# First mixture of experts: products in two halves of 32 slots, the second half and the shared block under three short branches

## The chip, the cores and the metric

The kernel runs on one core of one Trainium2 chip, in one launch. The metric is the device time of a launch in microseconds; the median of several runs counts. The core's engines are named as in the profile: PE is TensorE's matmuls (PEld its weight loads), DVE is VectorE, ACT ScalarE, POOL GpSimd, and SP SyncE, whose queue issues the weight transfers. A "q" behind an engine's name (PEq, SPq) is its sequencer. PSUM is where PE writes its results.

## The reference

The model has two layers over 256 context and 256 latent tokens of width 1024. Each layer ends in a mixture of 32 experts; every token goes to the two best experts of its group, and each expert is a gated MLP with a hidden width of 512:

```python
def run(args):
    xe, e = args
    return (jax.nn.silu(xe @ w_gate[e]) * (xe @ w_up[e])) @ w_down[e]
...
gates = gw * p_in / jnp.sum(p_in, axis=-1, keepdims=True)
eidx = grp[:, None] * MOE_PER_GROUP + e_in.astype(jnp.int32)
```

The first layer's mixture, which the change concerns, sees all 512 tokens, so 1024 pairs of token and expert; the second layer's sees the 256 latent tokens. How many tokens an expert gets is known only on the chip, from the router.

## The kernel before

**Slots.** The first mixture is `experts()`, called for layer 0. An expert has 64 slots. Tokens are put into them by a product with a one-hot matrix (`onehot`, `gather`, L1935), and the results are spread back to the tokens by another (`scatter`, L2002, then DVE at L2004 and L2006). What an expert has beyond 64 tokens goes to a shared block of 64 more slots `xx`; that block is computed with the weights of every expert that is too large, under a branch on the expert's flag (`shared`, L2197). A loop behind it (`others`) would take further shared blocks if one didn't do.

**One expert.** The order on each engine is the order in which the code is written. For expert e: `stage1` (L1958) multiplies the 64 gathered tokens by the gate and up weights, half of the depth at a time, each in a column group of 64 slots and 512 columns, with a piece of an earlier pair's scatter between the halves. Then comes the branch with `shared`. Behind it are `hidden` (silu on ACT, L1962, and the product with gate and up on DVE, L1963), the second product of expert e − 1 (`products`, `stage2`, L1979), `parts` (which splits its result into a high and a low part for an exact scatter: a copy on ACT, L1986, and a subtraction on DVE, L1987, twice), another piece of scatter, the transposes of the hidden values (`hidden_t`, L1971, L1973), a gather for the next group of four experts, and every second or fourth expert `turned` (L1993) and `gates_of` (L1947).

**Weights.** The `stream` holds tiles of 1 MiB in a ring; in this mixture it has 11 slots. An expert takes six: two of gate, two of up, two of down. `stream.give(n)` returns n tiles and lets SP ask for the next n in the plan. In `experts` this is `give(6)` after the second product; behind the last expert's tiles the plan goes on with the next layer's `od_w_in`.

**Branches.** A `tc.If` is run by every engine: it loads the flag (`values_load`), compares, and jumps over the body when the flag is zero. The branch at the last expert holds two more, nested: the shared block for expert 0, whose weights are long gone and are loaded again, and `others()` with loads for all 32 experts.

**Bookkeeping.** The flags are worked out on DVE in small steps (`bookkeeping`) during expert 0, in tiles borrowed from ones used later.

**The second mixture**, `narrow()`, is not touched. It has 32 slots for an expert and four column groups of 32 slots and 256 columns (L2287 first product, L2304 second), one short branch for an expert at L2501, and one large one at L2479.

Of the kernel before, what the change touches and what calls it, by code (L numbers as in the profile page):

```python
# [206 lines left out]
class Kernel:  # L207
# [1404 lines left out]
    def moe_tiles(self, NT):  # L1612
# [8 lines left out]
            extra=mp.tile([128, NE + 1 if NT > 2 else 3 * NE + 1], I32, name="extra"))  # L1621
# [196 lines left out]
    def bookkeeping(self, gp, lgg, mg, m1, m2, ohg, masked, chosen, oh1, oh2, slots, blocks):  # L1818
# [33 lines left out]
        nc.vector.tensor_reduce(over, counts.rearrange("p t e -> p e t"), axis=AX.X, op=ALU.add)  # L1852
        nc.vector.tensor_scalar(over, over, float(slots), 0.0, op0=ALU.subtract, op1=ALU.max)
# [20 lines left out]
        flags = gp.tile([128, extra.shape[1]], F32, name="flags")  # L1874
# [8 lines left out]
        nc.vector.tensor_tensor(flags[:, 0:NE], flags[:, 0:NE], over, op=ALU.mult)  # L1883
        n = self.most_blocks(NT, blocks)
# [3 lines left out]
        at = 0 if blocks > 1 else NE - 1  # L1888
        for v in (more[:, 0:1], flags[:, 1 - (at > 0):2 - (at > 0)]):
            nc.vector.tensor_tensor(flags[:, at:at + 1], flags[:, at:at + 1], v, op=ALU.max)  # L1890
# [7 lines left out]
    def experts(self, L, x, seg, bookkeeping, ending):  # L1898

        nc, tc, c, stream, I = self.nc, self.tc, self.c, self.stream, self.I  # L1900
# [4 lines left out]
        GB = 4  # L1905
        with ExitStack() as st:
# [4 lines left out]

            place = cycle([(wp, "xg"), (self.xp, "x01")] if L else [(wp, "xg"), (wp, "xh")])
# [28 lines left out]
            def gates_of(b):  # L1941

                g2 = self.m["gate2"]
                ps = pp.tile([128, GB // 2, 2, 2], F32, name="b2")
                for i in range(GB // 2):
                    for t in range(NT):
                        nc.tensor.matmul(ps[:, i].rearrange("p h e -> p (h e)"), OH[b][:, t, 2 * i:2 * i + 2].rearrange("p e s -> p (e s)"),  # L1947
                                         g2[:, :, t, b * GB + 2 * i:b * GB + 2 * i + 2],
                                         start=i == 0 and t == 0, stop=t == NT - 1, skip_group_check=True)
                GS[b] = wp.tile([128, GB], F32, name="gs")  # L1950
                for j in range(2):
                    nc.vector.tensor_reduce(GS[b][64:128, j::2], ps[64 * j:64 * j + 64, :, :, j], axis=AX.X, op=ALU.add)
# [7 lines left out]
            def hidden(ps, gs):  # L1960
                sg, hs = low[:, 0:FE], low[:, FE:].rearrange("p (k q) -> p k q", k=4)
                nc.scalar.activation(sg[64:128], ps[0:64], AF.Silu)  # L1962
                nc.vector.scalar_tensor_tensor(  # L1963
                    hs[64:128].rearrange("s k q -> s q k"), ps[64:128].rearrange("s (q k) -> s q k", k=4), gs,
                    sg[64:128].rearrange("s (q k) -> s q k", k=4), op0=ALU.mult, op1=ALU.mult)
                return hs

            def hidden_t(hs, ht, tag=dict(name="b2")):
                pt = pp.tile([128, 4, SLOTS], F32, **tag)
                for k in range(4):  # L1970
                    nc.tensor.transpose(pt[:, k], hs[64:128, k], c["ident"][64:128, 64:128])  # L1971
                ht = ht.rearrange("p (k s) -> p k s", k=4)
# [3 lines left out]
            def stage2(ps, ht, w, half):  # L1976
                for k in range(2 * half, 2 * half + 2):
                    for j in range(2):
                        nc.tensor.matmul(ps[64 * j:64 * j + 64], ht[:, k], w[:, k % 2, 512 * j:512 * j + 512],  # L1979
                                         start=k == 0, stop=k == 3)  # L1980
# [619 lines left out]
```

## Time and profile before

| | us |
|---|---|
| median of 3 runs (lowest to highest) | 1871.91 (1870.68 to 1872.27) |
| the profiled execution | 1874.16 |
| its span, first to last instruction | 1872.4 |
| PE busy | 1637.9 (87%) |
| DVE busy | 817.3 (44%) |
| ACT busy | 447.0 (24%) |
| POOL busy | 139.5 (7%) |
| mean granted clock of PE | 0.925 |
| DMA, mean over the span | 270 GB/s |

The span is cut by what the kernel does: the first mixture runs from about 600 to 1155 us, the second from about 1400 to the end. A row of a timeline reads: start, length, engine, line, operation, output<-inputs, shapes, count of instructions merged into the row, and in brackets how long the engine sat idle before it and what ended that. "PEq L2197" as the releaser means that PE's own sequencer was at the branch of line 2197.

### The profile page before, as it was taken

To read this page: it belongs to the slowest core of one execution; us is meant where nothing else is said; L and a number is where in the kernel's file an instruction comes from. 1 tells how busy PE (TensorE), PEld (TensorE's weight loads), DVE (VectorE), ACT (ScalarE), POOL (GpSimd) and SP (SyncE) were. 2 spreads that over 40 slices of the span, in tenths; PEclk is the share of its full clock that TensorE was granted. 3 is DMA by queue.
4 is the path that set the end of the run, shared out by engine and by line. 5 is a ranking of instruction groups with operands and counts; after the bars stand their busy time and mean duration, and the time that the engine had idled before them with its cause. 6 is when DMAs were issued, how large, how long until landed. Compare 5 with 4: busy or idle time off the path is not lost. (4 is left out here: it accounts for less than half of the span.)

```text
span 1872.4 us, 31604 instructions
## 1 busy us (share of the span) xinstructions
PE 1637.9 (87%) x12958; PEld 933.3 (50%) x12958; DVE 817.3 (44%) x1622; ACT 447.0 (24%) x945; POOL 139.5 (7%) x170
## 2 busy tenths in 40 slices
PE   5988999989998999999999997999987787776667
PEld 2755556454776444444444433888754333332222
DVE  2564434544358245555555456665562212221113
ACT  3442222421213211111111112544421111111001
POOL 1021000103115000000000003200010000000001
PEclk8998987879898999999999997999988899898888
DMA  9275300652243879999999990622699998999996
GB/s 319 82 239 191 113 24 23 216 172 92 85 146 141 350 283 386 399 385 390 390 401 379 399 386 12 198 68 85 259 369 413 415 415 318 414 414 414 366 400 253
DMA packets 127284, 505.76 MB, mean 270 GB/s; under 512 B 11317, under 2 KB 38945, under 8 KB 85986
## 3 DMA queue, kind: packets, MB, share of 16 engines
q1 hardware_dynamic: 120946, 493.96, 68.1%
q0 software_dynamic: 3488, 8.26, 1.4%
q8 instruction: 143, 2.34, 0.5%
q10 hardware_dynamic: 2640, 0.65, 0.2%
q14 instruction: 67, 0.55, 0.1%
HBM read 501.73 MB, written 1.10 MB: 269 GB/s over the span
## 5 line engine op out<-in xcount | busy, mean ns | idle before, releaser
L1979 PE MATMUL b<-w,ht 128*64 128x512 f32 x512 | 118.8, 604 | 8.6 <-PEq L2197 8.2
L2004 DVE TENSOR_TENSOR tmp<-b,g 128x512 f32<-128x512 f32 x128 | 87.6, 686 | 70.1 <-PE b L2002 69.2
L1958 PE MATMUL b<-w,xh 128*64 128x512 f32 x512 | 116.9, 599 | 0.0
L1958 PE MATMUL b<-w,xg 128*64 128x512 f32 x512 | 116.9, 599 | 0.0
L2287 PE MATMUL b<-w,x 128*32 128x256 f32 x1024 | 77.8, 430 | 31.7 <-DMA w<-moe_w_up 14.9
L2006 DVE TENSOR_TENSOR x<-x,tmp 128x512 f32<-128x512 f32 x124 | 90.1, 726 | 4.3
L2287 PE MATMUL b<-w,xg 128*32 128x256 f32 x1024 | 74.0, 420 | 19.1 <-DMA w<-moe_w_up 14.4
L1987 DVE TENSOR_TENSOR yl<-b,yh 64x512 fp32r<-64x512 f32 x62 | 42.7, 688 | 101.4 <-ACT yh L1986 101.4
L2304 PE MATMUL b<-w,ht 128*32 128x256 f32 x1024 | 71.2, 415 | 16.6 <-ACT ht L2299 12.4
L2292 DVE SCALAR_TENSOR_TENSOR low<-b,gs,low 64x256 f32<-64x256 f32 x32 | 15.7, 490 | 157.6 <-ACT low L2291 157.6
L1979 PEld LDWEIGHTS b<-w,ht 128*64 128x64 f32 x512 | 41.6, 138 | 84.0 <-issue 72.5
L1962 ACT ACTIVATE low<-b 64x512 f32<-64x512 f32 x33 | 19.4, 588 | 253.9 <-PEq L2197 221.0
L2453 DVE COPY y<-b 32x256 f32<-32x256 f32 x62 | 25.9, 418 | 119.6 <-PE b L2304 106.3
L2287 PEld LDWEIGHTS b<-w,x 128*32 128x32 f32 x1024 | 37.1, 122 | 69.5 <-DMA w<-moe_w_up 20.6
L1986 ACT CAST yh<-b 64x512 fp32r<-64x512 f32 x62 | 36.0, 581 | 127.8 <-PE b L1979 104.6
L1963 DVE SCALAR_TENSOR_TENSOR low<-b,gs,low 64x512 f32<-64x512 f32 x32 | 36.1, 1127 | 67.2 <-ACT low L1962 67.2
L1958 PEld LDWEIGHTS b<-w,xh 128*64 128x64 f32 x512 | 33.9, 136 | 62.6 <-issue 62.0
L1958 PEld LDWEIGHTS b<-w,xg 128*64 128x64 f32 x512 | 33.9, 136 | 62.3 <-issue 61.3
L2291 ACT ACTIVATE low<-b 64x256 f32<-64x256 f32 (+1 forms) x36 | 14.4, 399 | 209.9 <-PEq L2501 130.4
L2287 PEld LDWEIGHTS b<-w,xg 128*32 128x32 f32 x1024 | 36.0, 120 | 53.3 <-DMA w<-moe_w_up 19.5
L2002 PE MATMUL b<-yh,oht 128*128 128x512 f32 (+1 forms) x128 | 58.3, 456 | 3.2 <-DVE tmp L2004 3.2
L1374 PE MATMUL b<-w,hH 128*128 128x256 f32 x320 | 59.4, 286 | 0.0
(868 smaller groups left out, 3115.5 us busy)
## 6 DMA issues: line engine op xcount, KB each, us to landing
w<-moe_w_gate SPq DMA_DIRECT2D x128, 1024.0 KB
w<-moe_w_up SPq DMA_DIRECT2D x128, 1024.0 KB
w<-moe_w_down SPq DMA_DIRECT2D x128, 1024.0 KB
w<-ada_w SPq DMA_DIRECT2D x48, 1024.0 KB
w<-od_w_in SPq DMA_DIRECT2D x12, 1024.0 KB
w<-ev_w_in SPq DMA_DIRECT2D x8, 1024.0 KB
w<-ev_w_out SPq DMA_DIRECT2D x5, 1024.0 KB
w<-od_w_out SPq DMA_DIRECT2D x4, 1024.0 KB
```

The lines of the kernel that those rows point to most:

```text
L1374: nc.tensor.matmul(ps[:, t], l[:, k, T], r[:, k], start=t == 0 and k == 0 and i == 0, stop=k == 7 and i == 2, skip_group_check=True)
L1958: nc.tensor.matmul(ps[64 * j:64 * j + 64], xe(k), w[j][:, k % 4], start=k == 0, stop=k == 7)
L1963: nc.vector.scalar_tensor_tensor(hs[64:128].rearrange("s k q -> s q k"), ps[64:128].rearrange("s (q k) -> s q k", k=4), gs, sg[64:128].rea ...
L1979: nc.tensor.matmul(ps[64 * j:64 * j + 64], ht[:, k], w[:, k % 2, 512 * j:512 * j + 512], start=k == 0, stop=k == 3)
L1986: nc.scalar.copy(out=yh[:, j], in_=pj)
L1987: nc.vector.tensor_tensor(yl[:, j], pj, yh[:, j].bitcast(F32), op=ALU.subtract)
L2002: nc.tensor.matmul(ps, ohT[0:n, t], y[0:n, j], start=i == 0, stop=i == len(parts) - 1)
L2004: nc.vector.tensor_tensor(tmp, ps, g2[seg[t]][:, 512 * j:512 * j + 512], op=ALU.mult)
L2006: (nc.gpsimd if j in aside else nc.vector).tensor_tensor(xs, xs, tmp, op=ALU.add)
L2287: nc.tensor.matmul(ps[groups[j]], xe(k), w[j // 2][:, k % 4, 256 * (j % 2):256 * (j % 2) + 256], start=k == 0, stop=k == 7, skip_group_che ...
L2304: nc.tensor.matmul(ps[groups[j]], ht[:, k % 2, S * (k // 2):S * (k // 2) + S], w[:, k % 2, 256 * j:256 * j + 256], start=k == 0, stop=k == ...
L2453: (nc.scalar.copy if j % 2 else nc.vector.tensor_copy)(out=out, in_=ps[groups[j]])
```

## The change

In the first mixture an expert's 64 slots are computed as two halves of 32. The first half is always computed, in four column groups of 32 slots and 256 columns as in `narrow`. The second half is computed only for experts with more than 32 tokens. One count per expert says how far it goes: 0 for up to 32 tokens, 1 for more than 32, 2 for more than 64.

Three branches that are not nested stand in the body of an expert: the first product and hidden values of the second half (`size > 0`), the shared block (`size > 1`), and, after the gather, the transposes, second product and parts of the second half (`size > 0`). The hidden values of the first half are computed ahead of the branches. `parts` goes in four pieces of 32 rows and 256 columns, into tiles that stay and are set to zero once at the start. Weights are returned in two steps, four after the branches and two after the second product. The large branch with expert 0's shared block and `others()` moves from inside the last expert's branch to a branch of its own ahead of expert 29's first product. The bookkeeping is done in one go during expert 0. The down weights of this layer are read in the layout that the second mixture uses: two rows of 4 KB for a partition of a tile, where it was one of 8 KB.

```diff
-            [rows(I["moe_w_down"][L, e], 4, half) if L == 0 else
-             [(lambda w: w.rearrange("p (k f) -> p k f", k=2), I["moe_w_down"][L, e].rearrange("(k p) f -> p k f", k=4)[:, 2 * half:2 * half + 2])]
+            [[(lambda w: w.rearrange("p (k f) -> p k f", k=2), I["moe_w_down"][L, e].rearrange("(k p) f -> p k f", k=4)[:, 2 * half:2 * half + 2])]
...
+            nc.vector.tensor_scalar(flags[:, NE + 1:], over, NARROW + 0.5, None, op0=ALU.is_gt)
...
+            nc.vector.tensor_tensor(flags[:, NE + 1:], flags[:, NE + 1:], flags[:, 0:NE], op=ALU.add)
...
             def stage1(ps, xe, w, half, ks=range(4)):
                 for k in (4 * half + i for i in ks):
-                    for j in range(2):
-                        nc.tensor.matmul(ps[64 * j:64 * j + 64], xe(k), w[j][:, k % 4], start=k == 0, stop=k == 7)
+                    for j in range(4):
+                        nc.tensor.matmul(ps[groups[j]], xe(k), w[j // 2][:, k % 4, 256 * (j % 2):256 * (j % 2) + 256], start=k == 0, stop=k == 7,
+                                         skip_group_check=True)
...
-            def parts(ps, yh, yl):
+            def parts(ps, rows, yh, yl):
-                for j in range(2):
-                    pj = ps[64 * j:64 * j + 64]
-                    nc.scalar.copy(out=yh[:, j], in_=pj)
-                    nc.vector.tensor_tensor(yl[:, j], pj, yh[:, j].bitcast(F32), op=ALU.subtract)
+                for j in range(4):
+                    out = slice(256 * (j % 2), 256 * (j % 2) + 256)
+                    nc.scalar.copy(out=yh[rows, j // 2, out], in_=ps[groups[j]])
+                    nc.vector.tensor_tensor(yl[rows, j // 2, out], ps[groups[j]], yh[rows, j // 2, out].bitcast(F32), op=ALU.subtract)
...
+            rows = [[wp.tile([128, 2, 512], F32R, name=f"y{m}{i}", bufs=1) for m in "hl"] for i in range(2)]
+            nc.gpsimd.memset(low, 0.0)
+            for y in sum(rows, []):
+                nc.scalar.copy(out=y.rearrange("p j f -> p (j f)"), in_=low)
...
+                if e == NE - 3:
+                    with tc.If(flag(0) > 0):
+                        shared(0, loaded(0))
+                        others()
                 for half in range(2) if e else ():
-                    stage1(ps, xe, w[e][2 * half:2 * half + 2], half)
+                    stage1(ps, xe(0), w[e][2 * half:2 * half + 2], half)
...
+                hs = hidden(ps, gs(0), low[64:128, 0:256], low[64:128, 256:512])
+                size = flag(NE + 1 + e, 2)
+                with tc.If(size > 0):
+                    ps = pp.tile([128, 256], F32, name="b7")
+                    for half in range(2):
+                        stage1(ps, xe(1), w[e][2 * half:2 * half + 2], half)
+                    hidden(ps, gs(1), low[64:128, 512:768], low[64:128, 768:1024])
                 if e:
-                    with tc.If(flag(e) > 0):
-                        shared(e, lambda at, n: w[e][at:at + n])
-                        if e + 1 == NE:
-                            with tc.If(flag(0) > 0):
-                                shared(0, load(0))
-                            others()
-                hs = hidden(ps, GS[b][64:128, r:r + 1])
+                    with tc.If(size > 1):
+                        shared(e, resident(w[e]))
+                if not end:
+                    stream.give(4)
                 if e:
-                    products(e - 1)
-                    if e + 1 < NE:
-                        stream.give(6)
+                    ps = second(e - 1, ht.pop(e - 1), w.pop(e - 1))
+                    parts(ps, *part_rows(e - 1, 0))
+                    if not end:
+                        stream.give(2)
                     scatter(rows_of(late) if todo else (), todo[n:])
...
+                with tc.If(size > 0):
+                    ps = second(e, hidden_t(low[64:128, 768:1024], wp.tile([128, 512], F32, name="tmp")[:, 0:128].rearrange("p (k s) -> p k s", k=2)),
+                                w[e])
...
+                        parts(ps, *part_rows(e, 1))
```

**PE, expert 7.** From the second half of the first product to the second product of expert 6; the rows between a COMPARE and its UNCONDITIONAL_BRANCH are the body. Before:

```order
L1958 MATMUL b_6204<-w,xh 64x512 x8
L2112 TENSOR_LOAD extra
L2197 COMPARE_AND_BRANCH
L1958 MATMUL b_6248<-w,xx 64x512 x16
L1971 MATMUL b_6268<-const_ident,low 128x64 x4
L1979 MATMUL b_6274<-w,tmp 64x512 x8
L2197 UNCONDITIONAL_BRANCH x2
L1979 MATMUL b_6287<-w,ht 64x512 x8
```

The same place in the changed kernel:

```order
L1965 MATMUL b_6886<-w,xh 32x256 x16
L2127 TENSOR_LOAD extra
L2220 COMPARE_AND_BRANCH
L1965 MATMUL b_6948<-w,xh 32x256 x32
L2220 UNCONDITIONAL_BRANCH x2
L2226 COMPARE_AND_BRANCH
L2055 MATMUL b_6984<-w,xx 64x512 x16
L1976 MATMUL b_7006<-const_ident,tmp 128x64 x4
L2064 MATMUL b_7012<-w,tmp 64x512 x8
L2226 UNCONDITIONAL_BRANCH x2
L1983 MATMUL b_7031<-w,ht 32x256 x16
```

A matmul counted once here stands in the trace as two records. One body has become two, and a third (L2248) stands behind the gather; each half of the first product now counts 16 of 32 slots by 256 columns, not 8 of 64 by 512.

**ACT, expert 7.** From the branch to the copies behind the second product; `low` is where the silu goes, `yh` the high part, `ht` the transposed hidden values, `xg` the gathered tokens. Before:

```order
L2197 COMPARE_AND_BRANCH
L1962 ACTIVATE low<-b_6248 64x512
L1973 COPY tmp<-b_6268 128x256
L2197 UNCONDITIONAL_BRANCH x2
L1962 ACTIVATE low<-b_6204 64x512
L1986 CAST yh<-b_6287 64x512 x2
L1973 COPY ht<-b_6327 128x256
L1938 COPY xg<-b_6333 128x512
```

And changed, from the end of the second branch to the third:

```order
L2226 UNCONDITIONAL_BRANCH x2
L1990 CAST yh_5082<-b_7031 32x256 x4
L1977 COPY ht<-b_7073 128x128
L1943 COPY xg<-b_7077 128x512
L2248 COMPARE_AND_BRANCH
L1977 COPY tmp<-b_7097 128x128
L1990 CAST yh_5082<-b_7101 32x256 x4
L2248 UNCONDITIONAL_BRANCH x2
```

The expert's own silu now stands ahead of the first branch, and the copy of the second half's transposes (`tmp`) stands behind four copies of parts, the first half's `ht` and the gather's `xg`.

**SP, the last experts.** The weights' requests around the large branch. Before, at experts 30 and 31:

```order
L150 DMA w<-moe_w_up 128x2048
L150 DMA w<-moe_w_down 128x2048 x2
L150 DMA w<-od_w_in 128x8x256
L2112 TENSOR_LOAD extra
L2112 ISA x2
L2197 COMPARE_AND_BRANCH
L2112 TENSOR_LOAD extra
L2112 ISA x2
L2200 COMPARE_AND_BRANCH
L2107 DMA xg<-moe_w_gate 128x2048
```

Changed, from expert 28's requests to the start of the large branch's body:

```order
L150 DMA w<-moe_w_up 128x2048
L150 DMA w<-moe_w_down 128x2x1024 x2
L150 DMA w<-moe_w_gate 128x2048
L150 DMA w<-moe_w_up 128x2048
L150 DMA w<-moe_w_gate 128x2048
L2248 COMPARE_AND_BRANCH
L2248 UNCONDITIONAL_BRANCH x2
L2127 TENSOR_LOAD extra
L2127 ISA x2
L2209 COMPARE_AND_BRANCH
L2118 DMA xg<-moe_w_gate 128x1024
```

Before, all of the mixture's weights are asked for when SP comes to the branch with loads in its body; now nine tiles of experts 30 and 31 stand behind it.

## Rows read from the trace of the kernel before

**Rows 1.** Busy time by stretch: start:end, length, then each engine, clock, DMA share, GB/s.
```profile
700.00:1100.00 400.00, 394.22 (x1966) 181.07 (x1964) 202.96 (x304) 71.87 (x135) 0.00 (x0) 1.00 0.97 389
...
1600.00:1760.00 160.00, 110.97 (x1186) 53.66 (x1190) 33.70 (x75) 18.86 (x53) 0.00 (x0) 0.86 1.02 414
```

**Rows 2.** Timeline of PE, expert 7: start, us, engine, line, operation, count [idle].
```profile
731.43 3.65 PE L1958 MATMUL b<-w,xh 128*64 128x512 f32 x16
...
739.96 3.65 PE L1979 MATMUL b<-w,ht 128*64 128x512 f32 x16 [0.16 <-PEq L2197]
...
744.67 0.46 PE L1971 MATMUL b<-const_ident,low 64*128 64x64 f32 x4
...
747.93 3.65 PE L1958 MATMUL b<-w,xg 128*64 128x512 f32 x16
```

**Rows 3.** Timeline of ACT: the silu of experts 8 and 29.
```profile
756.39 0.59 ACT L1962 ACTIVATE low<-b 64x512 f32<-64x512 f32 x1 [8.55 <-PEq L2197]
...
1094.76 0.59 ACT L1962 ACTIVATE low<-b 64x512 f32<-64x512 f32 x1 [7.78 <-PEq L2197]
```

**Rows 4.** Timeline of PE, second mixture: first and second product of an expert.
```profile
1643.13 3.63 PE L2287 MATMUL b<-w,xg 128*32 128x256 f32 x64
...
1664.93 1.93 PE L2304 MATMUL b<-w,ht 128*32 128x256 f32 x32 [0.58 <-ACT ht L2299]
```

**Rows 5.** Timeline of DVE, second mixture: two copies that alternate with ACT.
```profile
1643.38 0.41 DVE L2453 COPY y<-b 32x256 f32<-32x256 f32 x1 [5.15 <-PE b L2304]
1644.23 0.42 DVE L2453 COPY y<-b 32x256 f32<-32x256 f32 x1 [0.43 <-ACT y L2453]
```

**Rows 6.** PE's waits, 690 to 1100 us: line, releaser, total, times, longest.
```profile
PE b L1979 <- PEq L2197: 4.7, 24, 0.3
```

**Rows 7.** PE's waits, 1400 to 1760 us, behind the second mixture's branch.
```profile
PE b L2265 <- PEq L2501: 11.5, 7, 4.6
...
PE b L2298 <- PEq L2501: 8.7, 4, 3.9
...
PE b L2319 <- PEq L2501: 5.2, 6, 3.5
```

**Rows 8.** Line 2479, second mixture's large branch: ns minimum/median/maximum, first, last start.
```profile
L2479 PEldq COMPARE_BRANCH  x1: 5977/5977/5977, 1744.1 to 1744.1; - x1
```

**Rows 9.** Timeline of PE in the shared block of expert 3.
```profile
669.35 0.46 PE L1971 MATMUL b<-const_ident,low 64*128 64x64 f32 x4 [1.88 <-DVE low L1963]
670.27 5.27 PE L1979 MATMUL b<-w,tmp 128*64 128x512 f32 x16 [0.46 <-ACT tmp L1973]
```

**Rows 10.** Second mixture's large branch: timeline of SP, then busy time by stretch.
```profile
1756.18 0.58 SPq L150 DMA_DIRECT2D w<-moe_w_up  x1
1778.74 0.34 SPq L150 DMA_DIRECT2D w<-moe_w_gate  x1
...
1770.00:1774.00 4.00, 2.88 (x36) 1.23 (x36) 0.57 (x2) 0.88 (x3) 0.00 (x0) 1.00 0.75 302
1774.00:1778.00 4.00, 0.86 (x8) 0.30 (x12) 0.76 (x2) 0.72 (x2) 0.00 (x0) 1.00 0.21 88
1778.00:1782.00 4.00, 1.68 (x28) 0.76 (x20) 0.00 (x0) 0.00 (x0) 0.00 (x0) 1.00 0.55 160
```

**Rows 11.** End of the first mixture: timeline of PE, then of SP.
```profile
1127.34 5.35 PE L1979 MATMUL b<-w,ht 128*64 128x512 f32 x16 [2.80 <-PEq L2197]
1132.62 0.50 PE L2002 MATMUL b<-yh,oht 128*128 128x512 f32 x1
...
1170.41 0.35 SPq L223 DMA_DIRECT2D const_rope_cos<-const_odd  x1
```

**Rows 12.** Ahead of the first expert: timelines of ACT and of POOL.
```profile
582.27 1.04 ACT L1730 CAST xh<-VU 128x1024 fp32r<-128x1024 f32 x1 [3.83 <-DVE ss L1718]
...
598.55 0.59 ACT L1938 COPY xg<-b 128x512 f32<-128x512 f32 x1 [2.47 <-PE b L1935]
...
594.24 0.94 POOL L2041 MEMSET low<- 64x1024 f32 x1
```

More of the change, by code (lines that the diff above doesn't have):

```diff
@@ L1904, in experts @@
         T = NT * 128
-        GB = 4
+        GB, S = 4, NARROW
+        groups = [slice(S * j, S * j + S) for j in range(4)]
         with ExitStack() as st:
@@ L1973, in hidden_t, with hidden @@
+            def hidden(ps, gs, sg, hs):
+                nc.scalar.activation(sg, ps[0:64], AF.Silu)
+                nc.vector.scalar_tensor_tensor(hs, ps[64:128], gs, sg, op0=ALU.mult, op1=ALU.mult)
+                return hs
+            def hidden_t(hs, ht, n=2, tag=dict(name="b2")):
+                pt = pp.tile([128, n, 64], F32, **tag)
+                for k in range(n):
+                    nc.tensor.transpose(pt[:, k], hs[:, 128 * k:128 * k + 128], c["ident"][64:128, 64:128])
                 nc.scalar.copy(out=ht, in_=pt)
@@ L2046, in shared @@
                 ps = pp.tile([128, FE], F32, name="b7")
-                for half in range(2):
-                    stage1(ps, lambda k: xx[:, k], w(2 * half, 2), half)
-                ht = hidden_t(hidden(ps, gx[64:128, e:e + 1]), wp.tile([128, 512], F32, name="tmp")[:, 0:256], dict(name="b7"))
+                for n in range(4):
+                    both = w(n)
+                    for k in range(2):
+                        for j, m in enumerate(both):
+                            nc.tensor.matmul(ps[64 * j:64 * j + 64], xx[:, 2 * n + k], m[:, k], start=n == 0 and k == 0, stop=n == 3 and k == 1)
+                sg, hs = (wp.tile([128, 512], F32, name="tmp")[64:128] for i in range(2))
+                hidden(ps, gx[64:128, e:e + 1], sg, hs)
+                ht = hidden_t(hs, wp.tile([128, 512], F32, name="tmp")[:, 0:256].rearrange("p (k s) -> p k s", k=4), 4, dict(name="b7"))
                 ps = pp.tile([128, 512], F32, name="b7")
                 for half in range(2):
-                    stage2(ps, ht, w(4 + half, 1)[0], half)
+                    down = w(4 + half)
+                    for k in range(2):
+                        for j in range(2):
+                            nc.tensor.matmul(ps[64 * j:64 * j + 64], ht[:, 2 * half + k], down[:, k, 512 * j:512 * j + 512],
+                                             start=half == 0 and k == 0, stop=half == 1 and k == 1)
                 for j in range(2):
@@ L2056, in back @@
             def back():
-                a, b = (xg(F32R) for i in range(2))
-                oht = a[:, 0:T].rearrange("p (t q) -> p t q", t=NT)
-                yh, yl = (v.rearrange("p (j f) -> p j f", j=2) for v in (a[:, T:T + 1024], b[:, 0:1024]))
-                nc.scalar.copy(out=yh[0:64], in_=yx)
-                nc.vector.tensor_tensor(yl[0:64], yx, yh[0:64].bitcast(F32), op=ALU.subtract)
-                turned(lambda t: ohx[:, t], SLOTS, oht)
-                scatter([(oht, yh, SLOTS), (oht, yl, SLOTS)], pieces)
+                oht = turned(lambda t: ohx[:, t], SLOTS, wp.tile([128, 2048], F32, name="xg", bufs=1)[:, 0:T].rearrange("p (t q) -> p t q", t=NT),
+                             dict(name="b7"))
+                scatter([(oht, yx, SLOTS)], pieces)
             def last_tokens():
@@ L2125, in others @@
                         for e in range(NE):
-                            shared(e, load(e))
+                            shared(e, loaded(e))
                         back()
-                    nc.gpsimd.memset(yx, 0.0)
+                    for _ in block(None):
+                        pass
             pieces = [(t, j) for t in range(NT) for j in range(2)]
```

135 lines of the change are left out of this document (67 added, 68 removed).

## Prediction

> **What bounds the kernel now.** I read the busy time by stretch first, since an average over the launch mixes stages with different limits. In 700 to 1100 us, most of the first mixture, the matmul engine is busy 394.22 of 400 us at granted clock 1.00 while the DMA engines move 389 GB/s. In 1600 to 1760, in the second mixture, whose experts already use 32 slots, it is busy only 110.97 of 160 us and the DMA moves 414 GB/s [rows 1]. So the first mixture is bound by matmuls, but a floor lies close below. An expert's weights are six tiles of 1 MiB; at 414 GB/s a tile takes 2.53 us and an expert 15.2. Experts 8 to 29 now take (1094.76 − 756.39) / 21 = 16.11 us each [rows 3]. Whatever matmul time the change takes away, no more than 0.9 us per expert can come back over a long stretch: 24 experts times 0.9 is 22 us, the ceiling.
>
> One expert on the matmul engine is read in its timeline: two stretches of 3.65 us for the first product (16 matmuls each, one row of the two stands), the skip of 0.16 us, 3.65 us for the second product, four transposes in 0.46, then the gather, and the next expert [rows 2].
>
> **How many experts are large.** Routing the reference's own inputs by its own formulas gives the tokens per expert of the first mixture: eleven have more than 32 (0, 1, 2, 3, 4, 6, 7, 11, 14, 19, 28), and only expert 3 more than 64. Seven of the eleven are among the first eight. So the change costs something at the start and pays afterwards.
>
> **A small expert.** With four column groups of 32 slots and 256 columns, the second mixture runs 64 first-product matmuls in 3.63 us and 32 of the second in 1.93 [rows 4], against 7.30 and 3.65 now. That is −3.67 and −1.72; half the transposes goes too, −0.2. Two more branches are skipped. The skip before the second product costs at most 0.3 now, 4.7 us in 24 [rows 6]; I take 0.35, +0.7 for two. 16.1 − 3.67 − 1.72 − 0.2 + 0.7 = **11.3 us** of matmul engine, so a run of small experts waits for DMA at 15.2.
>
> **A large expert.** It adds to that the second first product (+3.65) and second second product (+1.93), its transposes and copy (+0.5), saves two skips (−0.7), and waits. Inside the third branch the copy of the transposed hidden stands on the scalar engine behind the four copies of the parts, and each copy with its subtraction on the vector engine goes in turns: about 0.85 us from one to the next, as the second mixture's alternating copies do [rows 5]. 4 × 0.85 + 0.3 + 0.6 + half of 0.6 is 4.6 us after the second product; the scatter, gather and transposes that cover it take about 3.9; with the copy itself the wait is 1.2. Sum 11.3 + 3.65 + 1.93 + 0.5 − 0.7 + 1.2 = **17.9 us**, 1.8 more than now. Experts 0 to 2 have no scatter to cover the chain yet (about 1.1 to 1.9 more each), and expert 3 has half of it.
>
> **The first eight experts.** 3.7 + 3.6 + 3.1 + 2.9 + 1.8 (experts 0 to 4) − 4.8 (expert 5) + 1.8 + 1.8 = +14. After a wait the engine is slow for a while: behind an idle 1.88 us the 16 matmuls of 3.65 took 5.27 [rows 9]. On a second product of 1.93 that ratio is +0.85; I charge it five times, +4. The rows set to zero ahead of the first expert are a memset on GpSimd like the one of 0.94 at 594.24 and four scalar casts of 1.04 like that of 582.27. Begun at 594.24 they end at 594.24 + 0.94 + 4.16 = 599.3, and with the two short exponentials behind them at 599.8, where the first gather's copy now starts at 598.55 [rows 12]: +1, nothing if GpSimd is free earlier, 4 if the exponentials' users are late too. Expert 8, which begins at 747.93 now [rows 2], begins 19 us later, near 767.
>
> **From expert 8 to the end.** From here the DMA decides. Eleven tiles are requested ahead. At expert 8 the four tiles given back behind its branches are asked for at 767 + 3.65 + 1.1 + 0.7 = 772.4. By then 6 × 8 + 4 + 11 = 63 of the 192 are asked for. These four, some two still under way and the other 129 must land: 135 × 2.533 = 342 us, to 1114.4. The four large experts among them (17.9 against 15.2) run behind by 2.7 each and catch up inside the eleven tiles. The queue must also pass the large branch, now in front of expert 29. When the queue skips a body that holds DMAs, it first lets all that is under way land. In the second mixture this is seen: nothing is issued from 1756.18 to 1778.74, and the rate falls to 302, 88 and 160 GB/s in three stretches of 4 us [rows 10], which is (112 + 326 + 254) × 4 / 414 = 6.7, about 7 us of transfer lost. Before, this stood in expert 31, behind the last weights, and cost the weights nothing. The matmul engine's own skip of such a body, 5.98 us there [rows 8], lies within that. The last tile lands at 1121.4 and the second before it at 1116.3. The last first product, two skips and the second product of expert 30 then end at 1116.3 + 1.9 + 0.7 + 1.9 + 0.5 = 1121.3. Now that product ends at 1132.62, after an idle 2.80 and 5.35 us at the slow clock [rows 11]. That is −11.3. The tail gives back up to 1.8: four part pairs at 0.85 for two, and eight scalings of 32 rows for four of 64, on a vector engine that is busy there. **−9.5**: the profiled 1874.16 would be 1864.7, and since it stood 2.25 above the median, 1862.4 by the median, **1862**. The next layer's weights, whose requests move with the same ring, don't matter: the queue issues nothing more until 1170.41 [rows 11].
>
> The down weights are now read in rows of half the length. Both mixtures show a rate (389 and 414 [rows 1]), and the second reads all its down weights in that layout at 414, so I take no cost.
>
> **Rivals.** *The skips cost what they cost in the second mixture.* There the waits behind its branch were 11.5 us in 7, 8.7 in 4 and 5.2 in 6, up to 4.6 [rows 7]: 25.4 / 17 = 1.5 us each, 2.2 in one group. With s us per skip a small expert takes 10.2 + 3s, a large one 17.6 + s, the mean of experts 8 to 31 is 11.4 + 2.67s, which passes the DMA's 15.2 at s = 1.4; beyond it each further 0.1 us costs 6.4 us there and 0.7 at the start. The gain of 9.5 has shrunk to 2 at s = 1.4 and is gone near 1.43, the point that decides. At the first group's s = 1.64 the time is 15 us above now, 1887. For it: three branches, where one stood. Against: at this same place in the code the skip of the longer shared body costs 0.3 at most [rows 6], and the bodies are shorter now.
> The Trainium skill (Runtime: NRT & Kernel Launch, Instruction fetch mechanics) says that instructions are fetched ahead in sequence only, and that a branch taken to a target outside the fetched window waits for a fetch of its own. By it three branches per expert are three chances of such a stall, and a mean near the second mixture's would give this rival's 1887; the trace agrees for the large body (5.98), while the short skips of the first mixture show 0.3.
> *The first eight cost twice what I think*, by slow clock and by the chain of copies: expert 8 begins 28 us late instead of 19, and 0.5 us is left of the gain: no change, 1871. For it: every large expert has two waits, and the slow stretch of [rows 9] followed a wait of only 1.88. Against: with small waits between dense matmuls the clock stood at 1.00 over 400 us [rows 1].
> *The start is cheap.* If the chain is covered and the clock holds, expert 8 is some 8 us late, and if the large branch's loss is only 3 us: 1862 − 11 − 4 = 1847; half of that is 1854. For it: the chain's cover is counted to a few tenths.
> *The count doesn't sort the experts*, and every second half runs: 31 × 1.8 = +56, 1928; the thresholds are plain in the diff, so this is 1 in 100.
>
> **How the numbers follow.** Forecast (4 to 13 us faster) .45; cheap start (more than that) .17; no change .18; dear skips (with the miscount) .20. A measurement of this kernel tells about 0.2%, 3.7 us, from no change: faster .62, same .18, slower .20. The range runs from 1849 (most of the cheap start) to 1888 (dear skips at 1.64); beyond it lie the dearer skips and the cheapest start, some 2 in 10.
>
> **What would show it.** In the profile after: small experts paced at 15.2 with the matmul engine idle on weights, large ones near 18; expert 8's first product near 767; the skips' waits at the three branches under 0.4 each; a hole in the queue in front of expert 29 of some 20 us of issues and 7 of transfer; the product of expert 30 ending near 1121. I am wrong if small experts' pace is above 15.5 with no DMA wait, which is the skips, or if expert 8 starts after 776, which is the start.

## The result: 1881.88 us, slower by 0.6%

The changed kernel takes 1881.88 us in the median of 7 runs (1876.49 to 1885.44); the kernel before, run beside it, 1870.68 (1864.18 to 1875.03). The ratio is 1.0062, with a 95% interval of 1.0041 to 1.0083. The forecast was 1862, so the sign is wrong; 1881.88 lies inside the range of 1849 to 1888, in the part that belonged to the dear skips.

The profiled execution took 1881.88 with a span of 1879.8. The first stretch of [rows 1], two shorter ones of 80 us, and the place of the large branch in four steps (start:end, length, PE, PEld, DVE, ACT, POOL, granted clock, DMA share, GB/s):

```profile
700.00:1100.00 400.00, 322.71 (x3700) 200.26 (x3700) 215.40 (x424) 86.91 (x227) 0.00 (x0) 0.96 0.98 396
760.00:840.00 80.00, 67.06 (x794) 42.60 (x784) 46.80 (x99) 18.43 (x48) 0.00 (x0) 0.96 0.99 397
840.00:920.00 80.00, 65.36 (x767) 40.87 (x760) 46.04 (x88) 16.88 (x44) 0.00 (x0) 0.96 1.00 403
1092.00:1096.00 4.00, 3.28 (x32) 1.59 (x32) 0.00 (x0) 0.00 (x0) 0.00 (x0) 0.50 0.96 391
1096.00:1100.00 4.00, 2.68 (x12) 1.36 (x12) 0.99 (x2) 0.00 (x0) 0.00 (x0) 0.50 0.28 111
1100.00:1104.00 4.00, 3.39 (x48) 1.66 (x44) 2.18 (x4) 0.38 (x1) 0.00 (x0) 0.77 0.01 4
1104.00:1108.00 4.00, 3.70 (x52) 2.24 (x48) 1.25 (x3) 1.32 (x4) 0.00 (x0) 1.00 0.94 323
```

PE is busy 322.71 of 400 us where it was 394.22, and yet the DMA moves 396 GB/s where it moved 389, not 414. What PE waits for in the first mixture (600 to 1180 us; total, times, longest), in two executions of the changed kernel and then in the kernel before:

```profile
PE b L1983 <- issue: 17.6, 6, 4.0
PE b L1983 <- PEq L2226: 16.0, 16, 2.2
PE b L1983 <- DMA w<-moe_w_gate: 9.0, 9, 2.0
```

```profile
PE b L1983 <- issue: 14.7, 5, 3.5
PE b L1983 <- PEq L2226: 11.5, 13, 3.0
...
PE b L1983 <- DMA w<-moe_w_gate: 5.6, 6, 2.1
```

```profile
PE b L1979 <- PEq L2197: 8.2, 27, 2.8
```

"PEq L2226" is the second branch, the place that answers to [rows 6]: 16.0 us in 16, where before it was 8.2 in 27, 2.8 of them at the large branch. The waits put down to `moe_w_gate` stand at the same place: L1983 is the second product, which reads down weights and no gate weights, so its releaser there is doubtful. "issue" is the new kind, which no second product of the kernel before has: PE stops in the middle of a second product though data, buffers and weights are there. One such stop, in expert 15, behind its two skips:

```profile
874.28 0.63 PE L1983 MATMUL b<-w,ht 128*32 128x256 f32 x5 [0.74 <-DMA w<-moe_w_gate]
878.90 3.63 PE L1983 MATMUL b<-w,ht 128*32 128x256 f32 x27 [3.99 <-issue]
```

Five of the matmuls are done, then nothing for 3.99 us; the other 27 take 3.63 us where 32 take 1.93 (granted clock 0.50 from 878.90 to 882.50). In that gap of 4 us one packet of the queue of kind "instruction" lands, among the weights:

```profile
q8 instruction: 1, 0.02, 1.7%
```

And over 640 to 1080 us the same queue (count, MB, share) in the kernel before and in the changed one:

```profile
q8 instruction: 28, 0.46, 0.4%
```

```profile
q8 instruction: 59, 0.97, 0.9%
```

It fetches twice as many blocks of code; the queue's packet in the gap above ends at 877.56, 1.3 us ahead of PE's going on. The other five stops of the first list show the same: a block of 16 KB ends 1.3 to 1.5 us before PE goes on. So the changed kernel's own code comes in while the DMA moves about 400 GB/s of weights; that the bodies which are jumped over are what doubles it is tested below.

**Where the time stands.** I cut each profiled execution at the first gather's copy on ACT and at the first matmul behind the mixture (L1154); but for the rows set to zero ahead of it, the stretch between is the only one that the change touches (us of the profile's span).

| kernel | launch to first gather copy | first mixture | from there to the end |
|---|---|---|---|
| before | 598.55 | 567.89 | 705.96 |
| before, second profile | 597.54 | 568.28 | 708.68 |
| changed | 594.26 | 574.45 | 711.09 |
| changed, second profile | 594.98 | 570.95 | 713.97 |

The mixture is 3 to 7 us longer, where the sum had the whole 9.5 shorter: 12 to 16 us of the miss are here. The stretch behind it is about 5 us longer in code that nobody touched. The profiled executions of the kernel before took 1874.16 and 1876.30, 2 to 7 us more than its medians; what of the 11 us between the medians that accounts for, the profiles don't show.

### The profile page after: what moved, and what is told of

Its sections match the earlier page's. It is cut to its first block, busy times and chain, and to the rows that moved or that the text cites. A ratio compares the mean times of both kernels' runs of the same rounds, so it can differ in the third digit from the quotient of the medians.

```text
span 1879.8 us, 37749 instructions
## 1 busy us (share of the span) xinstructions
PE 1556.2 (83%) x15508; PEld 961.5 (51%) x15508; DVE 839.0 (45%) x1793; ACT 472.3 (25%) x1077; POOL 142.4 (8%) x173
## 5 line engine op out<-in xcount | busy, mean ns | idle before, releaser
L1991 DVE TENSOR_TENSOR yl<-b,yh 32x256 fp32r<-32x256 f32 x168 | 70.6, 420 | 168.5 <-ACT yh L1990 167.6
L1983 PE MATMUL b<-w,ht 128*32 128x256 f32 x1024 | 72.3, 414 | 50.0 <-issue 17.6
L1990 ACT CAST yh<-b 32x256 fp32r<-32x256 f32 x168 | 61.2, 364 | 195.2 <-PE b L1983 132.4
L1965 PE MATMUL b<-w,xg 128*32 128x256 f32 x1408 | 86.2, 381 | 9.8 <-DMA w<-moe_w_up 5.5
L1965 PE MATMUL b<-w,xh 128*32 128x256 f32 x1344 | 85.3, 397 | 9.6 <-PEq L2209 4.4
L2343 PE MATMUL b<-w,ht 128*32 128x256 f32 x1024 | 78.6, 450 | 16.8 <-ACT ht L2338 12.5
L2326 PE MATMUL b<-w,xg 128*32 128x256 f32 x1024 | 74.9, 426 | 20.8 <-DMA w<-moe_w_up 14.3
L2326 PE MATMUL b<-w,x 128*32 128x256 f32 x1024 | 73.6, 420 | 19.6 <-DMA w<-moe_w_up 5.9
L1983 PEld LDWEIGHTS b<-w,ht 128*32 128x32 f32 x1024 | 37.8, 116 | 82.9 <-issue 39.1
L1965 PEld LDWEIGHTS b<-w,xg 128*32 128x32 f32 x1408 | 45.5, 109 | 43.2 <-issue 9.8
L1965 PEld LDWEIGHTS b<-w,xh 128*32 128x32 f32 x1344 | 44.0, 113 | 44.5 <-issue 16.0
L2326 PEld LDWEIGHTS b<-w,xg 128*32 128x32 f32 x1024 | 37.2, 122 | 55.6 <-DMA w<-moe_w_up 18.9
L2330 ACT ACTIVATE low<-b 64x256 f32<-64x256 f32 (+1 forms) x36 | 14.4, 400 | 197.2 <-PEq L2540 111.4
L1969 ACT ACTIVATE low<-b 64x256 f32<-64x256 f32 x43 | 16.2, 376 | 183.1 <-PEq L2220 89.2
L2343 PEld LDWEIGHTS b<-w,ht 128*32 128x32 f32 x1024 | 34.5, 125 | 46.6 <-ACT ht L2338 17.2
```

The lines of the kernel that those rows point to most:

```text
L1965: nc.tensor.matmul(ps[groups[j]], xe(k), w[j // 2][:, k % 4, 256 * (j % 2):256 * (j % 2) + 256], start=k == 0, stop=k == 7, skip_group_che ...
L1969: nc.scalar.activation(sg, ps[0:64], AF.Silu)
L1983: nc.tensor.matmul(ps[groups[j]], ht[:, k % 2, S * (k // 2):S * (k // 2) + S], w[:, k % 2, 256 * j:256 * j + 256], start=k == 0, stop=k == ...
L1990: nc.scalar.copy(out=yh[rows, j // 2, out], in_=ps[groups[j]])
L1991: nc.vector.tensor_tensor(yl[rows, j // 2, out], ps[groups[j]], yh[rows, j // 2, out].bitcast(F32), op=ALU.subtract)
L2326: nc.tensor.matmul(ps[groups[j]], xe(k), w[j // 2][:, k % 4, 256 * (j % 2):256 * (j % 2) + 256], start=k == 0, stop=k == 7, skip_group_che ...
```

## The experiments

**Twice the same kernels.** The second profiles are in the table and the fences above.

> The changed kernel once more, for a second profile. If the 5 us that its first profile lost in the untouched second mixture's last expert belong to the shifted place of its instructions, they are there again, at the same matmuls; if they are chance, the stretch from the first mixture's end to the launch's end differs by some us between the two.

> The kernel before once more, for a second profile of it: how far the stretches that the change doesn't touch (launch to first gather, first mixture's end to launch's end) differ between two executions of the same code. If by some us, only the first mixture's own length may be compared between single profiles.

The loss in the last expert of the second mixture is there in both profiles of the changed kernel, at the same matmuls, and not in the kernel before. In the order before, changed, changed again:

```profile
1850.49 3.67 PE L2518 MATMUL b<-y,oht 96*128 96x512 f32 x8 [0.31 <-PEq L2501]
```

```profile
1855.95 5.37 PE L2557 MATMUL b<-y,oht 96*128 96x512 f32 x8 [3.13 <-PEq L2540]
```

```profile
1856.26 5.37 PE L2557 MATMUL b<-y,oht 96*128 96x512 f32 x8 [2.11 <-PEq L2540]
```

So it is not the chance of one execution. The other kernels speak for the place that these instructions have in the program: with the same matmuls unchanged, the wait is 2.4 to 2.9 us with all counts zero, with two branches, with one more branch in the kernel before and in that kernel without its large branch, and 0.3 to 0.7 in the six other kernels and in the second execution of the kernel before. The mixture of the kernel before repeats within 0.4 us, the changed one's differs by 3.5.

**All skipped, and no branches.** The first of the two keeps every instruction and sets the counts to 0; the second takes the three short branches and their bodies out; the large branch stays in both. Both leave out the second halves and the shared block.

```diff
-            nc.vector.tensor_scalar(flags[:, NE + 1:], over, NARROW + 0.5, None, op0=ALU.is_gt)
+            nc.vector.tensor_scalar(flags[:, NE + 1:], over, 1e9, None, op0=ALU.is_gt)
...
-            nc.vector.tensor_tensor(flags[:, NE + 1:], flags[:, NE + 1:], flags[:, 0:NE], op=ALU.add)
+            nc.vector.tensor_tensor(flags[:, NE + 1:], flags[:, NE + 1:], flags[:, 0:NE], op=ALU.mult)
```

> Changed kernel with every expert's count set to 0, so all three short branches stand where they stood and are always skipped: the second halves of the eleven large experts and the shared block of expert 3 are left out (not the first halves). With their matmuls gone the weights set the pace from the start: 181 tiles x 2.53 us behind the first request near 608, and 8 us of hole at the large branch, so the second product of expert 30 ends near 1085 instead of 1134. Theory 'code' (waits for instructions behind skipped bodies, 41 us of them in the mixture's trace, are what the forecast missed and are not hidden by the weights): 15 us or more slower than the run without branches, about 1845 to 1855. Theory 'place' (the large branch ahead of expert 29 and the slow matmul engine behind it cost the time; the short skips hide under the weights): about 1833 and within 5 us of the run without branches.

> The same with the three short branches and their bodies taken out of the code; the large branch stays ahead of expert 29. It leaves out the second halves and the shared block. Theory 'code': 15 us or more below the run with all counts zero, about 1830, and no waits for instructions of over 1 us inside the experts. Theory 'place': about 1830, within 5 us of it, with the hole ahead of expert 29 as in the changed kernel.

1840.24 us (ratio 0.9842, 0.9818 to 0.9866) and 1821.60 (0.9732, 0.9703 to 0.9762), against 1867.55 for the kernel before beside them. Same work, 18.6 us apart; in the profiles the mixture takes 536.98 and 514.85. The 18.6 us are the price of skipping 95 bodies where the weights were to hide it. PE's waits, first with all skipped, then without branches:

```profile
PE b L1983 <- DMA w<-moe_w_gate: 22.8, 12, 5.4
PE b L1965 <- DMA w<-moe_w_up: 20.8, 18, 1.9
PE b L1983 <- issue: 18.4, 7, 3.5
PE b L1983 <- PEq L2226: 17.0, 13, 3.8
```

```profile
PE b L1965 <- DMA w<-moe_w_up: 63.4, 39, 1.9
...
PE b L1965 <- issue: 3.6, 1, 3.6
```

```profile
q8 instruction: 31, 0.51, 0.5%
```

Without branches PE waits for weights and little else, which is what the forecast expected of small experts. All skipped, the waits in front of the second product, with those put down to `moe_w_gate`, come to about 46 us in 31, and the stops inside it to 18.4. From 640 to 1080 us, 31 blocks of code are fetched without branches and 64 with all skipped (shown below): code that is jumped over is fetched. In the middle the weights nearly hide this (412 GB/s against 416 from 760 to 920 us); at the start they don't (393 against 416 from 600 to 760), nor behind the last weights. Both times are some 5 to 8 us below what was expected, but the gap between them is that of the theory "code" (15 or more), not of "place" (5 at most). The pair alone doesn't tell the fetch from the branch itself.

**Small bodies.** The same counts of 0, the same three branches on the same engines, but 4, 2 and 6 matmuls in the bodies instead of 32, 28 and 18. The core of the edit:

```diff
                 with tc.If(size > 0):
                     ps = pp.tile([128, 256], F32, name="b7")
-                    for half in range(2):
-                        stage1(ps, xe(1), w[e][2 * half:2 * half + 2], half)
+                    for j in range(4):
+                        nc.tensor.matmul(ps[groups[j]], xe(1)(0), w[e][j // 2][:, 0, 256 * (j % 2):256 * (j % 2) + 256], start=True, stop=True,
+                                         skip_group_check=True)
```

> As the run with all counts zero (second halves and shared block left out), with the three branches and engines kept, but each skipped body cut to a few instructions: 4, 2 and 6 matmuls instead of 32, 28 and 18. Theory 'code' (what a skip costs is the fetch of instructions that are not yet there, which goes with the length of what is jumped over): within 6 us of the run without branches, 1822 to 1828. Theory 'branch' (loading the flag, draining the engines and raising the semaphores cost, whatever the body): as with the full bodies, 1836 to 1842.

1833.75 us (0.9820, 0.9802 to 0.9839; another chip than the pair above, so the ratios are compared: 0.9842, 0.9820, 0.9732). By the medians only a small part of the 18.6 us went, and the figure of neither theory is met. By the profile, whose execution was the fastest of the four at 1828.84, the mixture takes 523.62, which is 13.4 below the full bodies, whose profile was the slowest of its four (1846.51), and 8.8 above no branches. The waits say which part went; then the blocks of code, with small and with full bodies:

```profile
PE b L1965 <- DMA w<-moe_w_up: 58.1, 45, 3.4
PE b L1983 <- PEq L2227: 13.9, 19, 0.9
```

```profile
q8 instruction: 36, 0.59, 0.6%
```

```profile
q8 instruction: 64, 1.05, 1.0%
```

In front of the second product no wait is above 0.9 us but the last expert's (2.8, for the vector engine, as in the other kernels), the stops in the middle are gone, and 36 blocks are fetched where the full bodies take 64. What stays is about 0.73 us for each pair of skips, close to the 0.7 of the prediction. So the waits of 2 to 4 us come from the amount of jumped code. How much of the median they make stays open between the two readings.

**One more branch in the kernel before.** Its PE has no slack, so a skip shows at full price.

```diff
+                    with tc.If(flag(e, 2) > 1):
+                        shared(e, lambda at, n: w[e][at:at + n])
```

> The kernel before with one more branch in experts 1 to 31, behind the first: the flag loaded again, compared with more than 1, and a second copy of the shared block's code in its body, never taken. Nothing else changes, and the matmul engine sets the pace here, so the price of a skip shows undiluted. By the prediction's 0.35 us a skip: 11 us slower, about 1880. Theory 'code' (the sequencer often finds the instructions behind a skipped body not yet there): 0.6 to 1.3 us each, 18 to 40 us slower, 1887 to 1909, with waits of 2 to 4 us in some experts.

1903.43 us (1.0176, 1.0135 to 1.0217), 34.6 more than before.

```profile
PE b L1979 <- PEq L2203: 36.9, 31, 4.5
```

```profile
773.10 3.65 PE L1979 MATMUL b<-w,ht 128*64 128x512 f32 x16 [1.13 <-PEq L2203]
```

The price is in the range of "code", its form isn't: nearly every skip costs the same 1.0 to 1.3 us, the two loads and compares on end with 0.16 to 0.3 of it there before, and only one wait is long (4.5, in the last expert). A second branch with a flag of its own costs some 0.9 us by the waits, 1.1 by the medians, where nothing hides it. In 28 of the other 30 waits no block of code lands in the microsecond before them or in them, so that is the branch, not the fetch.

**Two branches instead of three, and one.** With two, the shared block's branch stands inside the third; with one, all three bodies stand behind the gather (the last expert keeps its three branches). The edit for two:

```diff
-                if e:
-                    with tc.If(size > 1):
-                        shared(e, resident(w[e]))
-                if not end:
-                    stream.give(4)
...
                 with tc.If(size > 0):
+                    if e:
+                        with tc.If(size > 1):
+                            shared(e, resident(w[e]))
                     ps = second(e, hidden_t(low[64:128, 768:1024], wp.tile([128, 512], F32, name="tmp")[:, 0:128].rearrange("p (k s) -> p k s", k=2)),
...
+                if not end:
+                    stream.give(4)
```

> Changed kernel with the shared block's branch moved inside the third one (more than 64 tokens implies more than 32), and the gate and up tiles returned behind it: a small expert skips twice, with its own second product, scatter and gather between the two jumps (32 matmuls' rows, then 46), where before 60 were jumped over in two branches on end. The work is the same. Theory 'code': fewer waits of 2 to 4 us, as the instructions jumped over at one place are half as many; the mixture 5 to 10 us shorter than the changed kernel's 571 to 574, 1872 to 1877. Theory 'volume' (it is the whole length of code to be brought in for an expert that counts, not how it is split): no gain, as with one branch, 1879 to 1885.

> Changed kernel with the three short branches of experts 0 to 30 made one, behind the gather: second half's first product, hidden values, shared block (nested in it), transposes, second product and parts; the gate and up tiles are returned behind it. The last expert keeps its three. A small expert skips once instead of three times. Theory 'code': about half the waits for instructions go, 6 to 12 us faster than the changed kernel, 1870 to 1876. Theory 'place': large experts wait about 1.5 us more on their hidden values (11 x 1.5, of which the seven early ones count), small ones gain nothing since they wait for weights: 0 to 10 us slower, 1882 to 1892.

Two: 1874.13 us (1.0031, 1.0014 to 1.0047), half of the loss gone by the middle of the intervals, which just overlap; the mixture takes 567.38, as before the change. One: 1882.22 (1.0076, 1.0054 to 1.0099), the mixture 574.03, nothing gained. By its time it lies in the range of "place", not of "code". PE's waits, with two, then with one:

```profile
PE b L1965 <- DMA w<-moe_w_up: 24.0, 20, 1.9
...
PE b L1983 <- PEq L2220: 4.7, 15, 0.4
...
PE b L1983 <- issue: 1.4, 1, 1.4
```

```profile
PE b L1965 <- PEq L2248: 22.6, 11, 5.8
...
PE b L1965 <- issue: 8.2, 7, 3.3
```

```profile
q8 instruction: 60, 0.98, 0.9%
```

With two, as much code is fetched (60 blocks for 59), but the jump of 60 matmuls in two bodies on end has become one of 32 and, a second product, a scatter and a gather later, one of 46. The waits at the second product fall from 16.0 to 4.7, the stops in it from 17.6 to 1.4. With one jump over all 78 the waits gather behind it, up to 5.8 us, and the large experts' transposes wait some 1.1 us each for their hidden values, as "place" had it. Between these three kernels, then, the length of one jump counts and not the volume. It isn't the only thing: the added branch above makes it 56 matmuls at one place, in two jumps with a load of the flag between, with less code in all (37 blocks), and there only one wait is long. Nor do the lumps explain the whole miss: with two branches they are gone, and the mixture is as long as before the change, not shorter by 9.5. In that run the large experts wait 16.4 us for the copy `tmp` where it was 9.0, and the gate and up tiles go back later.

**The large branch.** Moved back to the last expert, taken out of the changed kernel, and taken out of the kernel before (the last two leave out a reload and further blocks that this input doesn't need):

> Changed kernel with the large branch (expert 0's shared block and the further blocks) moved back to the last expert, behind its short branches, still not nested; all else as changed. Theory 'place': the hole of 8 us in the weights ahead of expert 29 goes, its skip of 6 us and the half clock behind it go from expert 29 and come back in part at expert 31: 8 to 14 us faster than the changed kernel, 1868 to 1874. Theory 'code': the waits behind the short branches stay, 0 to 4 us faster, 1878 to 1882.

> Changed kernel without the large branch; it leaves out the reload for expert 0 and the further shared blocks, which this input doesn't need, so the work done is the same. Theory 'large branch' (hole of 8 us in the weights, skip of 6 us and half clock behind it ahead of expert 29 lie on the path): 10 to 16 us faster than the changed kernel, 1866 to 1872. Theory 'short skips' (the last experts' chain on the matmul engine is late from the three skips of each, with nothing to hide them): 3 to 8 us faster, 1874 to 1879.

> The kernel before without its two nested branches in the last expert (the same work left out, not needed by this input). Both theories: the idle 2.80 us and the slow 5.35 us second product behind it go, 3 to 6 us faster than before. A gain of 10 or more would say that the large branch costs as much at its old place as at its new one.

1881.24 us (1.0069, 1.0045 to 1.0093), 1883.53 (1.0085, 1.0068 to 1.0102) and 1865.18 (0.9980, 0.9965 to 0.9996; 4 us, where 3 to 6 were expected). The mixtures take 574.40, 569.14 and 562.60 us. The theory "place" falls: without the large branch the hole in the weights is gone, but the median doesn't move; the 3 to 8 us of "short skips" aren't there either. In its place the changed kernel without it has these, in experts 29 and 30:

```profile
1097.94 1.70 PE L1983 MATMUL b<-w,ht 128*32 128x256 f32 x21 [3.30 <-issue]
...
1113.60 3.63 PE L1983 MATMUL b<-w,ht 128*32 128x256 f32 x29 [3.28 <-issue]
```

Two stops of 3.3 us in the second products that release the tiles for the last requests; behind the second the DMA moves 12 GB/s from 1112 to 1116. At the last expert the large branch costs as much as ahead of expert 29, by another wait, for the vector engine to come past it:

```profile
1132.72 4.00 PE L1983 MATMUL b<-w,ht 128*32 128x256 f32 x32 [6.47 <-DVEq L2224]
```

**Both halves always.** The first and the third branch removed, their bodies always run; the shared block's branch stays.

> Changed kernel with the first and the third branch removed and their bodies always run: both halves of 32 for every expert, only the shared block's branch left. This prices the large expert without skips. By the prediction's sum a large expert is 17.9 us against 16.1 before, so 31 x 1.8 = 56 us slower than before, about 1925. If the large expert was priced too low, which would be a rival cause of the missing gain, over 1940; if too high, under 1905.

1949.89 us (1.0429, 1.0384 to 1.0474). By the total the large expert was priced too low; by its pace it wasn't. The silu of two experts, eleven apart:

```profile
761.63 0.38 ACT L1969 ACTIVATE low<-b 64x256 f32<-64x256 f32 x1 [3.00 <-PE b L1965]
```

```profile
958.57 0.38 ACT L1969 ACTIVATE low<-b 64x256 f32<-64x256 f32 x1 [1.87 <-PE b L1965]
```

(958.57 − 761.63) / 11 = 17.9 us: the large expert was priced to the tenth. The 81 us are more than 31 × 1.8 = 56; the mixture alone is 642.31, 74 above before. Where the other 18 lie, at its first experts or its end, I haven't followed.

## Why the prediction was wrong, step by step

**The small expert (11.3 us).** Right as work, though its terms add up to 11.2. Experts 13 and 14 are 12 us apart in the changed kernel (silu at 843.37 and 855.34), with 1.35 us of wait at the skips between them, and without branches PE waits for weights throughout.

**The large expert and the first eight.** Right. 17.9 us is measured, and expert 8 began when it should:

```profile
594.26 0.57 ACT L1943 COPY xg<-b 128x512 f32<-128x512 f32 x1
```

```profile
762.22 1.93 PE L1965 MATMUL b<-w,xg 128*32 128x256 f32 x32
```

762.22 − 594.26 = 168.0 us behind the first gather's copy, where it was 747.93 − 598.55 = 149.4 [rows 2, 12]: 18.6 later, and 0.7 for the zeroing of the rows (from the router's first copy to the gather's 14.4 us, where it was 13.7): 19.3, forecast 19. The rival of a start twice as dear falls, and so does the cheap start.

**The weights from expert 8 on (414 GB/s).** Off by some 10 us. The rate is 397 and 403 over 760 to 920 instead of 414, which is (17 + 11) × 80 / 414 = 5.4, and 0.8 more in the 160 us behind. From 767 on 142.35 MB of weights land, 0.75 of a tile more than the 135 of the sum (1.9 us), and 1.01 MB of code blocks share the rate (2.4 us). A tile is asked for when the second product has released one, and the stops stand in front of and inside just that product; that they cost the 6 us of rate is argued, not shown. With two branches, where they are nearly gone, the rate over the same two stretches is 389 and 412; with all skipped, where they are all there, 414 and 410.

**The large branch's hole (7 us).** Right to 1 us: (23 + 303 + 410 + 91) × 4 / 414 = 8.0 from 1092 to 1108, and 21.5 us without a request:

```profile
1081.74 0.44 SPq L150 DMA_DIRECT2D w<-moe_w_gate  x1
1103.22 0.34 SPq L150 DMA_DIRECT2D w<-moe_w_up  x1
```

But its price was not the step: taking it out of the changed kernel doesn't move the median.

**The end (second product of expert 30 at 1121.3).** Here the sum failed most. It ended at 1134.13, 539.9 behind the first gather's copy where the sum had 521.7 (1121.3 less 599.6, where it had that copy): 18 us late. PE's last experts, from the large branch on:

```profile
1092.72 3.64 PE L1965 MATMUL b<-w,xh 128*32 128x256 f32 x32 [4.36 <-PEq L2209]
1097.68 0.77 PE L2006 MATMUL b<-yh,oht 128*128 128x512 f32 x1 [1.32 <-DVEq L2209]
...
1103.25 1.93 PE L1983 MATMUL b<-w,ht 128*32 128x256 f32 x32 [0.61 <-PEq L2226]
...
1118.39 0.39 PE L2006 MATMUL b<-yl,oht 128*128 128x512 f32 x1 [1.97 <-issue]
...
1121.51 3.64 PE L1965 MATMUL b<-w,xh 128*32 128x256 f32 x32
...
1133.14 1.06 PE L1983 MATMUL b<-w,ht 128*32 128x256 f32 x14 [1.58 <-issue]
1134.13 0.50 PE L2006 MATMUL b<-yh,oht 128*128 128x512 f32 x1
...
1143.16 3.41 PE L1983 MATMUL b<-w,ht 128*32 128x256 f32 x32 [2.80 <-DVEq L2248]
```

Before, it was 1132.62 [rows 11]. I took the product to end 5 us behind the tile two before the last. Some 12 of the 18 us are that tile's: the last up tile is the seventh of those asked for from 1103.22 on, and from about 1104.9 (323 GB/s in 1104 to 1108), with no pause in the rate,

```profile
1108.00:1128.00 20.00, 15.56 (x146) 8.29 (x142) 12.45 (x21) 3.09 (x9) 0.00 (x0) 0.83 1.02 413
```

seven tiles at 2.53 us land by 1122.6, an estimate from these rows. By the sum's own steps the product would then have ended at 1127.6. The other 6 or 7 us are PE's. From 1092.72 on it waits for no weights. Waits of 1.32, 0.61, 0.30, 0.56, 0.60, 0.75, 1.97, 0.42, 0.76 and 1.58 us add up to 8.9, and matmuls at the half clock behind them (3.64 for 1.93 twice, 2.98 for 1.93, and the scatter; granted clock 0.50 from 1092 to 1100 and from 1121.5 to 1125) to some 5 more. Of these 14 us the late weights hide about half; the forecast charged 0.7 for two skips. The wait of 2.80 at the last second product, for the vector engine to come past the third branch, stands where there was none.

**The skip at 0.35 us.** The step that failed. The mean was not far off: 17.6 + 16.0 us over 72 skips are 0.5 each, 0.6 with the 9.0 put down to `moe_w_gate`, far below the 1.4 at which the rival of dear skips was to decide. But they come in lumps of 1.4 to 4 us at about every second expert, some with slow matmuls behind, and a lump at the start or in the last experts isn't hidden. I divided by a mean and hid the quotient under the weights; all skipped against no branches, 18.6 us weren't hidden. The rows of the second mixture showed lumps of up to 4.6 [rows 7]; [rows 6] showed one jump over one body of 28 matmuls, and the bodies are not shorter now, as I wrote, but 32 and 28 on end. The rival had the right mechanism. That its 1887 lies near the 1881.88 measured, and that the range held the result, is luck: with skips of 0.6 us its own sum still gains some 8 us. The Trainium skill (Runtime: NRT & Kernel Launch, Instruction fetch mechanics) says that a branch taken out of the fetched window waits for a fetch; the runs agree for jumps over 60 matmuls and more, with 1.4 to 5.8 us. The short ones, at about 0.35 us each, show no such wait.

**What stays open.** How the 18.6 us between all skipped and no branches divide between fetch and branch: the profile of the small bodies gives the larger part to the fetch, its median the larger part to the branch. And the 5 us behind the mixture: the stalls at equal matmuls tie part of them to the place of the code, but no run moved that place alone. Last, the 9.5 us that the sum promised: the run without the lumps doesn't bring them. No version that was run beats the kernel before and handles every input.

## What to carry to other kernels

A skipped body isn't free: its code was fetched with the rest here, so price a branch also by how much is jumped over at one place, try to split long jumps by work that always runs, and put rare bodies inside a branch that is already there. Look at the start and the end of a stage apart: what weights hide in its middle stands bare there. And cut two profiles at marks that the change doesn't touch before explaining a difference of five microseconds.

## What the runs showed of the hardware that I had not expected

Stops without any wait in the middle of a run of matmuls, 1.6 to 4 us long, with a block of code landing 1.3 to 1.5 us before each of the six ends; code for a stage more than doubled (28 to 59 blocks in 440 us) by bodies that mostly don't run; and a change in one loop after which such stops come or go in code 700 us later, where the same matmuls waited 0.31 us before and 3.13 and 2.11 after.
